# An encoder block on one NeuronCore: the input projection in seven block products, its side work put into 224 slots by hand

## The chip, the core and the metric

The kernel runs on one core of a Trainium2 chip. The metric is the device time of one execution in microseconds; the kernel before took 1524.46 us (median of three runs, 1522.24 to 1525.68). Engines: TensorE (matmul, PE in the profile, its weight loads PEld), VectorE (DVE), ScalarE (ACT), GpSimd (POOL), SyncE (SP, which issues most DMAs). SBUF is the memory that the engines work in, PSUM holds TensorE's sums in banks of 128 x 512 float32, HBM lies outside.

## The reference, cut to what matters

One block over 2048 tokens of width 1024, all in float32:

```
u    = rms_norm(x, norm_in_g)
proj = u @ w_in                                # (2048, 1024) @ (1024, 4096)
pool_x, pool_z, m_x, m_z = split(proj, 4)      # 1024 columns each
y_pool = pool_mixer(pool_x) * silu(pool_z)     # window means 2, 4, 8, 16, then a 256x256 map per group
c = silu(conv5(m_x) + b);  q, k = headwise(c); v = headwise(m_x)
h = mlstm(q, k, v, gates, forward) + mlstm(..., backward)   # 4 heads, 16 chunks of 128 tokens
y_m = (norm(h) * w + skip * c) * silu(m_z)
out = rms_norm(x + concat(y_pool, y_m) @ w_out, norm_out_g)
```

## The kernel before, in words

Each float32 operand of the projection is split into two reduced-precision parts, hi and lo (`split`, line 89: a cast on ScalarE, a subtraction on VectorE, line 94), and each product is three matmuls: hi x hi, hi x lo, lo x hi.

**Projection** (`project`, line 129). The 4096 columns are 32 blocks of 128, the tokens 4 blocks of 512, the inner width 8 pieces of 128. One (column block, token block) is 24 matmuls into one of four PSUM banks (`psp`). The norm isn't multiplied into x: hi and lo of x times the norm's weight are made as the pieces arrive (lines 217, 218), and `rnorm` is multiplied in when a bank is read (lines 204, 408, 543, 550). So the first matmul needs one piece of x, and the norm of a token block (`squares`, `norm`, `spread`, lines 222 to 248) is needed when its first bank is read.

**Stages.** (1) `load_block` and the first two m_x column blocks. (2) The other six, with the mapping of m_x beside them: `conv` (line 311; five taps on VectorE), Silu, `headwise` (keys and values by token, lines 321 to 340; their transposes, line 344), and `fold` (line 162), which multiplies the pooling map into the pool_x weights. (3) Four m_z blocks with the gate rows. (4) Eight pool_x and eight pool_z blocks with the window sums. (5) The last four m_z blocks with the 15 updates of the backward state of head 0 (`next_backward`, line 622; `update`, line 593, which writes two PSUM banks of one buffer and has VectorE read them) and, in the last pair, the loads of the first half of w_out (`load_out`, line 636). (6) `run` (line 959): 64 steps of the memory with the output projection beside them.

**Order.** In stages 1 to 5 a planner orders each engine's instructions by its own estimate of when they can start. In stage 6 TensorE, VectorE, ScalarE and GpSimd keep the order of the program (`manual_schedule`, line 993); DMA queues are planned throughout.

Of the kernel before, what the change touches and what calls it, by code (L numbers as in the profile page):

```python
# [17 lines left out]
P = 128  # L18
# [3 lines left out]
NB = 4  # L22
# [8 lines left out]
ENG = mybir.EngineType  # L31

# [18 lines left out]
def hymba_block(ctx, tc, xT, x, w_in, wpxT, pool_w, bqT, bkT, bvT, bv, w_g, b_g, par, edge, w_out, g_out, out):  # L51
# [16 lines left out]
    g_s = dram.tile([2, P, P], F32, name="g_s")  # L68
    o_s = dram.tile([S, D], F32, name="o_s")
# [13 lines left out]
    dec_bc = cpool.tile([P, P], F32, name="dec_bc")  # L83
    pga = ExitStack()
# [11 lines left out]

    ph1 = ExitStack()
    rp = open_pool(ph1, "rp", side="right")
    wpool = open_pool(ph1, "wpool", bufs=2, side="right")
    psp = open_pool(ph1, "psp", bufs=4, side="right", space=PSUM)  # L100
    rnorm = rp.tile([P, S], F32, name="rnorm")
    uh, ul = {}, {}
    ub = {b: ExitStack() for b in reversed(range(NB))}
    for b, stack in ub.items():
        up = open_pool(stack, f"u{b}", side="right")
        uh[b] = up.tile([P, KT, BT], F32R, name=f"uh{b}")
        ul[b] = up.tile([P, KT, BT], F32R, name=f"ul{b}")

    def fetch_w(src):
        wl = wpool.tile([P, KT, P], F32, name="wl", bufs=1)  # L110
        nc.sync.dma_start(out=wl, in_=src)
        return wl

    def split_w(wl):
        whi = wpool.tile([P, KT, P], F32R, name="whi")
        wlo = wpool.tile([P, KT, P], F32R, name="wlo")
        split(wl, whi, wlo, nc.vector)
        return whi, wlo

    def load_w(src):  # L120
        return split_w(fetch_w(src))
# [7 lines left out]
    def project(w, b, kts=range(KT), ps=None):  # L129
        whi, wlo = w  # L130
        if ps is None:
            ps = psp.tile([P, BT], F32, name="proj")
        for kt in kts:
            for n, (l, r) in enumerate(((whi, uh[b]), (whi, ul[b]), (wlo, uh[b]))):
                pe(nc.tensor.matmul(ps, lhsT=l[:, kt, :], rhs=r[:, kt, :],  # L135
                                    start=(kt == 0 and n == 0), stop=(kt == KT - 1 and n == 2)))
        return ps


    phw = ExitStack()  # L140
    hwp = open_pool(phw, "hwp", bufs=2, side="right")

    def load_headwise(i):
        t = {}
        for name, src in (("k", bkT), ("v", bvT)):
            t[name] = hwp.tile([P, P], F32, name=f"bl{name}")
            nc.sync.dma_start(out=t[name], in_=src[i])

        t["q"] = hwp.tile([P, P + 48], F32, name="blq")
        nc.sync.dma_start(out=t["q"][:, :P], in_=bqT[i])  # L150
        nc.sync.dma_start(out=t["q"][:, P:].rearrange("p (a b) -> p a b", a=3), in_=w_g[i])
        t["vw"] = hwp.tile([P, 16 + P], F32, name="vw")
        nc.sync.dma_start(out=t["vw"][:, 16:], in_=bv[i])
        return t

    pm = ExitStack()
    mxp = open_pool(pm, "mxp", bufs=2)
    psk = open_pool(pm, "psk", bufs=3, space=PSUM)
    psg = open_pool(pm, "psg", space=PSUM)


    def fold(g):
        pwh = fop.tile([P, 2, HD], F32R, name="pwh", bufs=1)
        pwl = fop.tile([P, 2, HD], F32R, name="pwl", bufs=1)
        for ct in range(2):
            pw = fop.tile([P, HD], F32, name="wt", bufs=2)
            nc.sync.dma_start(out=pw, in_=pool_w[g][:, ct, :])
            split(pw, pwh[:, ct, :], pwl[:, ct, :], nc.gpsimd, nc.gpsimd)

        def parts(kt):  # L170
            wt = fop.tile([P, 2, P], F32, name="wt", bufs=2)
            nc.sync.dma_start(out=wt, in_=wpxT[g][:, :, kt * P:(kt + 1) * P])
            wh = fop.tile([P, 2, P], F32R, name="wh")
            wl = fop.tile([P, 2, P], F32R, name="wlf")
            split(wt, wh, wl, nc.gpsimd, nc.gpsimd)
            return wh, wl

        nxt = parts(0)
        yield
        for kt in range(KT):  # L180
            wh, wl = nxt
            ps = psk.tile([P, 2, P], F32, name="hw")
# [4 lines left out]
            st = fop.tile([P, 2, P], F32, name="st", bufs=1)  # L187
            nc.scalar.copy(st, ps)
            nc.scalar.dma_start(out=wp_s[2 * g:2 * g + 2, :, kt, :].rearrange("c p n -> p c n"), in_=st)
            if kt + 1 < KT:  # L190
                nxt = parts(kt + 1)
            yield

    def new_mx(pool):
        mx = pool.tile([P, S + 4], F32, name="mx")
        nc.gpsimd.memset(mx[:, :2], 0.0)
        nc.gpsimd.memset(mx[:, S + 2:], 0.0)
        return mx

    ws, hw, mxs = [], [], []  # L200

    def evac_mx(i, b, ps):
        bt = slice(b * BT, (b + 1) * BT)
        nc.vector.tensor_tensor(mxs[i][:, 2 + b * BT:2 + (b + 1) * BT], ps, rnorm[:, bt], op=ALU.mult)  # L204

    with ExitStack() as pro:
        xq = open_pool(pro, "xq", bufs=2)


        def load_block(b):  # L210
            xts = []
            for kt in range(KT):
                g = par_sb[:, kt, 9:10]
                xt = xq.tile([P, BT], F32, name="xt", bufs=12)
                xts.append(xt)
                nc.sync.dma_start(out=xt, in_=xT[b][:, kt, :])
                nc.scalar.activation(uh[b][:, kt, :], xt, AF.Copy, scale=g)
                nc.vector.scalar_tensor_tensor(ul[b][:, kt, :], in0=xt, scalar=g,  # L218
                                               in1=uh[b][:, kt, :].bitcast(F32), op0=ALU.mult, op1=ALU.subtract)
                yield xts  # L220

        def squares(xts):
            sm = None
            for k in range(KT // 2):
                sq = [xq.tile([P, BT], F32, name="sq", bufs=6) for e in range(2)]
                nc.gpsimd.tensor_tensor(sq[0], xts[2 * k], xts[2 * k], op=ALU.mult)
                nc.scalar.activation(sq[1], xts[2 * k + 1], AF.Square)
                (nc.gpsimd if k < 2 else nc.vector).tensor_tensor(sq[0], sq[0], sq[1], op=ALU.add)
                if sm is not None:
                    nc.vector.tensor_tensor(sq[0], sq[0], sm, op=ALU.add)  # L230
                sm = sq[0]
            return sm

        def norm(b, sm):
            ss = psg.tile([P, 512], F32, name="pg")
            for i in range(4):
                nc.tensor.matmul(ss[:, i:i + 1], lhsT=sm[:, i * P:(i + 1) * P], rhs=ones[:, 0:1], start=True, stop=True)
            rs = mxp.tile([P, 4], F32, name="rs")
            nc.vector.tensor_scalar(rs, ss[:, 0:4], 1.0 / D, EPS, op0=ALU.mult, op1=ALU.add)
            nc.gpsimd.tensor_tensor(rs, rs, mhalf, op=ALU.pow)  # L240
            return rs

        def spread(b, rs):
            rb = psg.tile([P, BT], F32, name="pg")
            for i in range(4):
# [10 lines left out]
        for b in range(NB):  # L256
            load = load_block(b)
            pss = [psp.tile([P, BT], F32, name="proj") for i in range(2)]
            for kt in range(KT):
# [12 lines left out]
                if kt == 3 and late:  # L272
                    late.pop()()
# [775 lines left out]
```

## Time and profile before

| | |
|---|---|
| three runs | 1522.24, 1524.46, 1525.68 us |
| profiled execution | 1520.88 us, its span 1519.2 us |
[...]
| projection (stages 1 to 5) | until 859 us of the span |

The page gives the busy time of each engine and the chain of work that ended last. A matmul's own duration (0.39 us for 512 columns) overlaps the next one's; the distance from start to start is its pitch. A row of the timeline gives start, duration, engine, line, operation, tiles and, in brackets, how long the engine was idle before it and who ended that. "x4" merges four instructions.

### The profile page before, as it was taken

The numbers are of one execution on the slowest core, as the hardware profiler recorded it, in microseconds if no ns is written. First come the engines' busy times: TensorE is split into PE (matmuls) and PEld (weight loads), VectorE is DVE, ScalarE is ACT, GpSimd is POOL, SyncE is SP. The second block draws the span as 40 slices with busy tenths as digits, with TensorE's granted clock in tenths as the row PEclk, the third lists the DMA queues.
The fourth block names the chain that finished last, engine by engine and source line by source line (L and its number), as shares of the span: only waits on it lengthen the run. The fifth ranks groups of instructions, "written<-read, shape, count | busy, mean of one in ns | idle before, by whom it ended". The sixth has DMA issues, their size and how long they took to land.

```text
span 1519.2 us, 21070 instructions
## 1 busy us (share of the span) xinstructions
PE 1493.2 (98%) x7193; PEld 1259.9 (83%) x7193; DVE 845.6 (56%) x1700; ACT 494.6 (33%) x1144; POOL 359.8 (24%) x549
## 2 busy tenths in 40 slices
PE   8899999999999999999999999999999999999998
PEld 6788888878888888888888878888888888888886
DVE  8896355563133333445433377767777777665553
ACT  6344433343110011011112444444344445433331
POOL 5544333310000210222200123233332323121100
PEclk8999999999999999999999999999999999999999
DMA  6268765552201111111053787877777778765442
GB/s 223 66 201 234 211 181 169 167 164 80 77 14 56 56 44 53 56 56 44 26 159 107 225 245 233 234 228 207 224 223 216 222 211 262 200 194 156 139 135 84
DMA packets 251339, 231.11 MB, mean 152 GB/s; under 512 B 18400, under 2 KB 211168, under 8 KB 250208
## 3 DMA queue, kind: packets, MB, share of 16 engines
q1 hardware_dynamic: 236768, 215.08, 47.9%
q10 hardware_dynamic: 14464, 14.68, 3.0%
q8 instruction: 57, 0.93, 0.3%
q14 instruction: 50, 0.41, 0.1%
HBM read 149.81 MB, written 79.89 MB: 151 GB/s over the span
## 4 chain that ended last, share of the span: by engine, by line
PE 91%; DVE 3%; DMA 3%; ACT 1%; POOL 1%; issue 1%; SPq 0%; DVEq 0%; POOLq 0%; ACTq 0%
PE proj L135 42%; PE po L685 23%; PE upd L597 7%; PE num L817 7%; PE hw L336 4%; PE num L812 4%; PE sT L802 2%; PE hw L185 1%; PE py L869 1%; DVE ul L218 1%; PE hw L344 1%; DVE c L316 1%; DMA kk<-kk_s 1%; DMA xt<-in_xT 1%; DMA wost<-in_w_out 1%
## 5 line engine op out<-in xcount | busy, mean ns | idle before, releaser
L135 PE MATMUL proj<-uh,whi 128*128 128x512 f32 x1024 | 407.7, 398 | 3.7 <-DVE mx L204 2.3
L135 PE MATMUL proj<-ul,whi 128*128 128x512 f32 x1024 | 402.3, 393 | 2.1 <-DVE ul L218 2.1
L135 PE MATMUL proj<-uh,wlo 128*128 128x512 f32 x1024 | 402.5, 393 | 0.0
L135 PEld LDWEIGHTS proj<-uh,whi 128*128 128x128 f32 x1024 | 194.4, 190 | 43.1 <-DVE mx L204 2.4
L135 PEld LDWEIGHTS proj<-ul,whi 128*128 128x128 f32 x1024 | 194.1, 190 | 41.8 <-DVE ul L218 2.4
L135 PEld LDWEIGHTS proj<-uh,wlo 128*128 128x128 f32 x1024 | 193.9, 189 | 41.2
L685 PE MATMUL po<-woh,yh 128*128 128x512 f32 x512 | 217.6, 425 | 0.0
L685 PE MATMUL po<-woh,yl 128*128 128x512 f32 x512 | 201.5, 394 | 0.0
L685 PE MATMUL po<-wol,yh 128*128 128x512 f32 x512 | 201.3, 393 | 0.0
L597 PE MATMUL upd<-v,kw 128*128 128x258 f32 x480 | 124.2, 381 | 3.1 <-ACT hh L833 1.9
L791 POOL TENSOR_TENSOR cw<-cT,gw 128x512 f32<-128x512 f32 (+1 forms) x64 | 79.0, 1234 | 168.5 <-issue 77.9
L685 PEld LDWEIGHTS po<-woh,yl 128*128 128x128 f32 x512 | 96.2, 188 | 22.1
L685 PEld LDWEIGHTS po<-wol,yh 128*128 128x128 f32 x512 | 96.6, 189 | 19.2
L685 PEld LDWEIGHTS po<-woh,yh 128*128 128x128 f32 x512 | 96.4, 188 | 19.1
L91 ACT CAST whi<-wl 128x1024 fp32r<-128x1024 f32 x31 | 32.6, 1052 | 229.0 <-PE proj L135 225.9
L316 DVE SCALAR_TENSOR_TENSOR c<-mx,par_sb,c 128x512 f32<-128x512 f32 x128 | 103.6, 827 | 3.0
L597 PEld LDWEIGHTS upd<-v,kw 128*128 128x128 f32 x480 | 87.3, 190 | 14.9 <-ACT hh L833 2.0
L543 DVE TENSOR_TENSOR ux<-proj,rnorm 128x512 f32<-128x512 f32 x32 | 22.1, 692 | 124.7 <-PE proj L135 124.7
L784 POOL TENSOR_SCALAR_AFFINE_SELECT gw<-gw 128x128 f32<-128x128 f32 x128 | 43.8, 365 | 172.6 <-DMA gw<-g_s 170.5
L875 ACT ACTIVATE yt<-cT,par_sb 128x128 f32<-128x128 f32 x128 | 44.5, 394 | 108.8 <-DMA ym_s<-yt 108.7
L851 POOL TENSOR_TENSOR rstd<-rstd,mhalf 128x1 f32<-128x1 f32 x64 | 35.1, 549 | 174.5 <-DVE rstd L849 99.8
L833 ACT ACTIVATE hh<-num,rn 128x256 f32<-128x256 f32 x64 | 30.1, 471 | 141.9 <-DVE rn L829 133.8
(194 smaller groups left out, 2184.5 us busy)
## 6 DMA issues: line engine op xcount, KB each, us to landing
gw<-g_s SPq DMA_DIRECT2D x128, 128.0 KB, 4.8
v<-v_s SPq DMA_DIRECT2D x124, 129.0 KB, 4.5
kk<-kk_s SPq DMA_DIRECT2D x124, 128.0 KB, 4.0
wl<-in_w_in SPq DMA_DIRECT2D x23, 512.0 KB, 3.8
xt<-in_xT SPq DMA_DIRECT2D x32, 256.0 KB, 4.8
cT_s<-c SPq DMA_DIRECT2D x32, 256.0 KB, 3.7
kk_s<-tokst SPq DMA_DIRECT2D x32, 256.0 KB, 2.5
kkT_s<-kkTb SPq DMA_DIRECT2D x32, 256.0 KB, 4.1
```

What stands on the lines that cost most here:

```text
L91: nc.scalar.copy(hi, src)
L135: pe(nc.tensor.matmul(ps, lhsT=l[:, kt, :], rhs=r[:, kt, :], start=(kt == 0 and n == 0), stop=(kt == KT - 1 and n == 2)))
L316: nc.vector.scalar_tensor_tensor(c, in0=mx[:, b * BT + t:(b + 1) * BT + t], scalar=par_sb[:, i, t:t + 1], in1=c, op0=ALU.mult, op1=ALU.add)
L336: nc.tensor.matmul(ps[:, e, :], lhsT=src[:, o:o + P], rhs=rhs, start=True, stop=True)
L597: pe(nc.tensor.matmul(ps[:, m, :E], lhsT=t["kw"][:, ms], rhs=t["v"], start=True, stop=True))
L685: pe(nc.tensor.matmul(ps, lhsT=l[:, kt, :], rhs=r, start=(kt == 0 and e == 0), stop=(kt == 7 and e == 2)))
L784: nc.gpsimd.affine_select(out=a["gw"][:, 0, d, :], in_=a["gw"][:, 0, d, :], compare_op=ALU.is_ge, fill=BIG, base=0, pattern=[[pat, P]], ch ...
L791: eng.tensor_tensor(a["cw"][:, ds], a["cT"][:, None].broadcast_to([P, nd, 2, P]), a["gw"][:, 1, ds, None, :].broadcast_to([P, nd, 2, P]), ...
L812: pe(nc.tensor.matmul(num[:, d, :E], lhsT=a["dd"][:, d, :], rhs=a["kv"]["v"], start=True, stop=d not in a["dirs"]))
L817: pe(nc.tensor.matmul(num[:, d, :E], lhsT=a["cw"][:, d, m, :], rhs=state[:, m, :], start=False, stop=(m == 1)))
L851: nc.gpsimd.tensor_tensor(a["rstd"][:, 0:1], a["rstd"][:, 0:1], mhalf[:, :1], op=ALU.pow)
L875: nc.scalar.activation(a["yt"][:, m, :], a["cT"][:, m, :], AF.Copy, scale=par_sb[:, i, 8:9])
```

## The change

The tokens become two halves of two blocks of 512, the inner width two halves of 512, and two column blocks are taken together: a 2x2x2 of blocks. Such a unit needs eight block products; seven products of sums and differences (P1 to P7) give the same four result blocks. There are 16 units (`plan`: four m_x pairs, one m_z pair, eight pool pairs (x and z of one block), three m_z pairs) in each of two halves of the tokens: 2 x 16 x 7 = 224 slots of one product (12 matmuls) each. P1, P6, P7 and P4 add up in one bank, P5 and P3 in another, P2 stands alone; banks are read in the slot after their product, three of them copied (`snap`) to be added elsewhere.

The combinations of x (seven operands of 512 x 512, hi and lo) stay in SBUF for a half: 14 tiles. So that they can be formed, the norm is now multiplied into x first (`scale_x`). The combinations of weights are made for every unit in both halves, sums on GpSimd, hi on ScalarE, lo on VectorE. All other work is attached to slots (`at_slot`): "top", "pre", "mid" (between the second and third quarter of the product) and "end". Four engines keep this order throughout. Convolution and pooling run in halves with a halo kept over (`mt_s`, `uxt`, `szt`); the second half maps its tokens in chunks of 384. The maps `mv` go to HBM and come back in the second half. `fold` splits with ScalarE and GpSimd where it used GpSimd alone, and `ob` has four buffers where it had two.

```diff
+    PRODUCTS = ("P1", "P5", "P6", "P2", "P7", "P3", "P4")
+    def load_raw(u):
...
+            raw[u, e] = ap.tile([P, KT, P], F32, name=f"w{e}")
+            nc.sync.dma_start(out=raw[u, e], in_=t)
+    def sum_a(u, k):
...
+        nc.gpsimd.tensor_tensor(sums[k], x, y, op=op_)
+    def prepare_a(u, k):
...
+        split(v[k] if k in v else sums[k], hi, lo, nc.vector)
+    def product(k, put, middle):
...
+        bank = "x" if k == "P2" else "z" if k in ("P5", "P3") else "y"
...
+        for q in range(4):
+            if q == 2:
+                middle()
+            for n, (l, r) in enumerate(((ah, bh), (ah, bl), (al, bh))):
+                pe(nc.tensor.matmul(ps, lhsT=l[:, q, :], rhs=r[:, q, :], ...
+        if k in ("P1", "P5", "P6"):
+            pending.append(lambda: snap(k, ps))
+        elif k == "P4":
+            pending.append(lambda: put(1, 0, ps, None))
+        else:
+            e, t, other = {"P2": (0, 0, "P1"), "P7": (1, 1, "P5"), "P3": (0, 1, "P6")}[k]
+            pending.append(lambda: put(e, t, ps, snaps[other]))
+    def squares(t, kt):
+        sq = ob.tile([P, BT], F32, name="op")
+        nc.scalar.activation(sq, xs[t, kt], AF.Square)
...
+            nc.vector.tensor_tensor(rn[t], rn[t], sq, op=ALU.add)
+    def scale_x(t, kt):
+        nc.vector.scalar_tensor_tensor(xs[t, kt], in0=xs[t, kt], scalar=par_sb[:, kt, 9:10], in1=rn[t], ...
+    def prepare_b(k):
...
+        for q in range(4):
+            x11, x12, x21, x22 = xs[0, q], xs[1, q], xs[0, 4 + q], xs[1, 4 + q]
+            v = {"P1": x11, "P5": x11, "P6": x11, "P2": x21, "P7": x12, "P3": x22, "P4": x21}[k]
+            if k in ("P5", "P6", "P7", "P4"):
+                x, y = {"P5": (x12, x11), "P6": (x22, x11), "P7": (x22, x12), "P4": (x21, x11)}[k]
+                (nc.vector if k in ("P5", "P6") else nc.gpsimd).tensor_tensor(v, x, y, op=ALU.subtract)
+            split(v, hi[:, q], lo[:, q], nc.vector)
+    SUMS = {3: "P5", 4: "P6", 5: "P7", 6: "P3"}
+    NEXT = {3: ("P1",), 4: ("P5",), 5: ("P6", "P2"), 6: ("P7",)}
+    OWN = {0: "P3", 1: "P4"}
+    def slot(g):
...
+        run_events(g, "top")
...
+        read_banks()
+        if k in OWN:
+            prepare_a(u, OWN[k])
+        if nxt and k == 1:
+            load_raw(nxt)
+        if nxt and k in SUMS:
+            sum_a(nxt, SUMS[k])
+            for x in NEXT[k]:
+                prepare_a(nxt, x)
+        run_events(g, "pre")
+        product(PRODUCTS[k], puts[U], lambda: run_events(g, "mid"))
+        run_events(g, "end")
...
+            for s, c in zip(range(6) if p else (0, 1, 3, 5), chunks):
+                at_slot(g + s, "pre", conv, p, *c)
+                at_slot(g + s + 1, "pre", conv_silu, p, *c)
+                at_slot(g + s + 2, "mid", headwise, p, *c, 0)
+                at_slot(g + s + 2, "end", headwise, p, *c, 1)
+                at_slot(g + s + 3, "mid", keys_across, p, *c)
...
+    E0 = UNITS * SLOTS
+        at_slot(E0 - 12 + kt // 2, "pre", squares, 1, kt)
+        at_slot(E0 - 7 + kt // 4, "pre", scale_x, 1, kt)
...
+    for k, s in zip(PRODUCTS, (1, 3, 4, 5, 7, 9, 10)):
+        at_slot(E0 - 7 + s, "pre", prepare_b, k)
+    for s in range(6):
+        at_slot(s, "end", fold_steps, 2)
...
+    schedule = tc.manual_schedule(engines={ENG.PE, ENG.DVE, ENG.Activation, ENG.Pool})
+    with schedule:
+        fold_steps(1)
...
+        load_x(xq[0], 0, 0)
+        load_raw(plan[0])
+        load_x(xq[1], 0, 1)
+        for kt in range(KT):
+            squares(0, kt)
+            fold_steps(1)
+        norm_sums(xq[0], 0)
+        norm_spread(0)
+        prepare_a(plan[0], "P1")
+        for k in ("P5", "P6", "P7"):
+            sum_a(plan[0], k)
+        for kt in range(4):
+            scale_x(0, kt)
+        prepare_b("P1")
+        for kt in range(KT):
+            squares(1, kt)
+        norm_sums(xq[1], 1)
+        norm_spread(1)
+        fold_steps(2)
+        for kt in range(4):
+            scale_x(1, kt)
+        for k in ("P5", "P6", "P2", "P7"):
+            prepare_a(plan[0], k)
...
+        for g in range(2 * E0 - 15):
+            slot(g)
...
+        for g in range(2 * E0 - 15, 2 * E0):
+            k = g - (2 * E0 - SLOTS)
+            if k < 0:
+                slot(g)
                 next_backward()
+                next_backward()
+                continue
...
+            slot(g)
+            bstack[PRODUCTS[k]].close()
+            room(k)
```

In the first slots `prepare_b` of P5, P6, P2 with P7, and P3 with P4 stand in slots 0, 1, 2 and 3; the other eight `scale_x` stand behind P5's in slot 0. `room` opens the SBUF that the closed operands leave, and loads and splits the first quarter of w_out and the first y there.

## Rows read from the trace of the kernel before

**Rows 1.** The page: busy time by engine, then the last chain by engine.
```profile
PE 1493.2 (98%) x7193; PEld 1259.9 (83%) x7193; DVE 845.6 (56%) x1700; ACT 494.6 (33%) x1144; POOL 359.8 (24%) x549
...
PE 91%; DVE 3%; DMA 3%; ACT 1%; POOL 1%; issue 1%; SPq 0%; DVEq 0%; POOLq 0%; ACTq 0%
```

**Rows 2.** Windows: length, PE, PEld, DVE, ACT, POOL busy, clock, DMA share, GB/s.
```profile
400.00:500.00 100.00, 100.00 (x443) 82.81 (x442) 32.89 (x30) 11.97 (x16) 7.61 (x8) 1.00 0.12 40
```

**Rows 3.** Timeline of projection alone: start, duration, engine, line, operation.
```profile
500.13 0.39 PE L135 MATMUL proj<-ul,whi 128*128 128x512 f32 x1
...
505.57 0.39 PE L135 MATMUL proj<-ul,whi 128*128 128x512 f32 x1
```

**Rows 4.** Timeline of TensorE: 12 fold products; 8 values, 4 transposes, projection again.
```profile
200.69 0.28 PE L185 MATMUL hw<-pwh,wh 128*128 128x256 f32 x1
...
202.12 0.39 PE L135 MATMUL proj<-uh,whi 128*128 128x512 f32 x1
...
205.86 1.14 PE L336 MATMUL hw<-vw,mx 128*128 128x144 f32 x8
206.84 0.60 PE L344 MATMUL hw<-ident,tokst 128*128 128x128 f32 x4
207.20 0.48 PE L135 MATMUL proj<-uh,whi 128*128 128x512 f32 x1
207.52 0.39 PE L135 MATMUL proj<-ul,whi 128*128 128x512 f32 x1
```

**Rows 5.** Windows of line 135 alone, then line 336 alone: the first 100 us.
```profile
0.00:100.00 100.00, 71.28 (x264) 53.95 (x264) 0.91 0.49 153
...
0.00:100.00 100.00, 4.11 (x30) 3.89 (x31) 0.91 0.49 153
```

**Rows 6.** Start: timeline of TensorE, then a window (PE busy, clock, DMA, GB/s).
```profile
10.50 0.63 PE L135 MATMUL proj<-uh,whi 128*128 128x512 f32 x1
10.93 0.63 PE L135 MATMUL proj<-ul,whi 128*128 128x512 f32 x1
...
10.00:15.00 5.00, 5.00 (x13) 0.51 1.05 396
```

**Rows 7.** Timeline of the first norm: power, spread.
```profile
27.12 1.46 POOL L240 TENSOR_TENSOR rs<-rs,mhalf 128x4 f32<-128x4 f32 x1 [1.36 <-DVE rs L239]
...
32.41 1.05 PE L246 MATMUL pg<-ident,rs 128*128 128x128 f32 x8
```

**Rows 8.** Groups by form: busy, mean ns of one, idle before: two lo parts.
```profile
L94 POOL TENSOR_TENSOR wlf<-wt,wh 128x256 fp32r<-128x256 f32 x32 | 30.6, 955 | 2.6
...
L94 DVE TENSOR_TENSOR wol<-wost,woh 128x512 fp32r<-128x512 f32 x32 | 23.0, 721 | 17.0 <-ACT woh L91 14.7 <-DMA sz_s<-op 2.2
```

**Rows 9.** Timeline: VectorE alone, and beside a GpSimd operation; three scalings alone.
```profile
19.42 0.68 DVE L230 TENSOR_TENSOR sq<-sq 128x512 f32<-128x512 f32 x1
19.57 1.42 POOL L226 TENSOR_TENSOR sq<-xt 128x512 f32<-128x512 f32 x1 [1.89 <-DVE sq L228]
20.02 1.52 DVE L228 TENSOR_TENSOR sq<-sq 128x512 f32<-128x512 f32 x1
...
59.60 2.06 DVE L218 SCALAR_TENSOR_TENSOR ul<-xt,par_sb,uh 128x512 fp32r<-128x512 f32 x3
```

**Rows 10.** Convolution: line 316 (ns min/median/max), and the group of its first step.
```profile
L316 DVE SCALAR_TENSOR_TENSOR c<-mx,par_sb,c x128: 733/753/1226, 75.7 to 314.5; 128x512 f32<-128x512 f32 x128
...
L314 DVE TENSOR_SCALAR c<-mx,par_sb 128x512 f32<-128x512 f32 x32 | 18.2, 573 | 9.9 <-PE hw L336 5.2 <-DMA wt<-in_wpxT 3.5 <-ACT c L318 0.8
```

**Rows 11.** Timeline: an update that waited for the one before; line 603's reading.
```profile
881.14 1.14 PE L597 MATMUL upd<-v,kw 128*128 128x258 f32 x4 [1.20 <-DVE cb L600]
...
L603 DVE SCALAR_TENSOR_TENSOR cb<-cb,dec_bc,upd x56: 741/752/753, 771.2 to 1247.0; 128x516 f32<-128x516 f32 x56
```

**Rows 12.** Timeline of ScalarE: a cast that waited for its load.
```profile
872.96 0.62 ACT L91 CAST woh<-wost 128x512 fp32r<-128x512 f32 x1 [3.80 <-DMA wost<-in_w_out]
```

**Rows 13.** Waits of TensorE: total us, times, longest.
```profile
PE hw L336 <- ACT tokst L337: 3.6, 3, 2.1
```

More of the change, by code (lines that the diff above doesn't have):

```diff
@@ L94, in split @@
         lo_eng.tensor_tensor(lo, src, hi.bitcast(F32), op=ALU.subtract)
-    ph1 = ExitStack()
[L98 to L121, printed above, removed]
+    PRODUCTS = ("P1", "P5", "P6", "P2", "P7", "P3", "P4")
+    keep = ExitStack()
+    kp = open_pool(keep, "kp")
+    uxt = kp.tile([P, 8, 16], F32, name="uxt")
+    szt = kp.tile([P, 8, 8], F32, name="szt")
+    ed = kp.tile([P, len(EDGE)], F32, name="ed")
+    nc.sync.dma_start(out=ed, in_=edge.partition_broadcast(P))
+    ph1 = ExitStack()
+    ap = open_pool(ph1, "ap", side="right")
+    psp = open_pool(ph1, "psp", side="right", space=PSUM)
+    bstack = {k: ExitStack() for k in reversed(PRODUCTS)}
+    bpool = {k: open_pool(stack, f"b{k}", side="right") for k, stack in bstack.items()}
+    B, A, raw, sums = {}, {}, {}, {}
     ordered = []
@@ L127, in pe @@
         return tc.keep_in_program_order(ins) if ordered else ins
[L129 to L137, printed above, removed]
@@ L140, in hymba_block @@
[L140 to L154, printed above, removed]
@@ L181, in fold @@
             wh, wl = nxt
+            if kt + 2 < KT:
+                load(kt + 2)
+            if kt + 1 < KT:
+                nxt = parts(kt + 1)
             ps = psk.tile([P, 2, P], F32, name="hw")
@@ new lines, in put_mx, with put @@
+    def put_mx(p, u):
+        def put(e, t, ps, other):
+            i = 2 * u[1] + e
+            if i not in made:
+                new_mx(p, i)
+                made.add(i)
+            a = at(p, p * S // 2 + t * BT)
+            dst = mxs[i][:, a:a + BT]
+            if other is None:
+                nc.scalar.copy(dst, ps)
+            else:
+                nc.vector.tensor_tensor(dst, ps, other, op=ALU.add)
+            if p == 0 and t == 1:
+                nc.sync.dma_start(out=mt_s[i], in_=mxs[i][:, FIRST:])
+        made = set()
+        return put
@@ new lines, in hymba_block, with open_m, open_z, open_x @@
+    left = {}
+    def open_m(p):
+        nonlocal mxp, sp, hwp
+        pm = left["m"] = ExitStack()
+        hwp = open_pool(pm, "hwp", bufs=2, side="right")
+        mxp = open_pool(pm, "mxp")
+        sp = open_pool(pm, "sp")
+    def open_z():
+        nonlocal zp
+        left["z"] = ExitStack()
+        zp = open_pool(left["z"], "pp", bufs=2)
+    def open_x(t):
+        left["x", t] = ExitStack()
+        xq[t] = open_pool(left["x", t], f"xq{t}")
+    def fold_steps(n):
+        for _ in range(n):
+            next(folds, None)
```

630 lines of the change are left out of this document (351 added, 279 removed).

## The prediction

> **What bounds the kernel now.** Read the page first: busy time, then the chain that ended last. TensorE is busy 98% of the span and the chain runs on it for 91%, on VectorE for 3% [rows 1]. Busy time overstates a pipelined engine, so look next at a stretch with projection alone: 100 us hold 443 products of 512 columns at clock 1.00 [rows 2], and the timeline there has 24 from one start to the next like it in 5.44 us, 0.2267 us each [rows 3]. VectorE, ScalarE and GpSimd have 33, 12 and 8 us of work in those 100 us [rows 2]. So before 860 us the time is the number of products times their pitch, plus what TensorE does between them, plus its waits. Most of the waits are at the front: in the first 100 us it issues 264 projection products (59.8 us) and 30 for keys and values (3.7 at 0.98/8) [rows 4, 5], and by their pitches 12 folds (1.4) [rows 4] and 64 norm products (8.4 at 1.05/8) [rows 7]; 73 of 100 us, so 27 are lost, partly to waits and partly to the half clock after them (pitch 0.43, granted clock 0.51) [rows 6].
>
> **The change, part by part.** Times are against the profiled execution, 1520.9 us (span 1519.2), which lies 3.6 below the median of the three runs, 1524.5; at the end I add 3.6.
>
> *Products.* Before: 32 column blocks x 4 token blocks x 8 x 3 = 3072. After: 16 pairs x 2 halves x 7 products x 12 = 2688. 384 x 0.2267 = **-87.1 us** [rows 3]. TensorE does everything else as often as before. Their pitch stays: same operands, banks of the same size, weight loads still under them.
>
> *The front.* Before, the first product needs one raw piece of x, and the norm is multiplied in on the way out. After, it needs the whole norm of 512 tokens, and the second product that of 1024. Step by step. (a) x, two weights and the first fold pieces are some 5.3 MB; at 396 GB/s [rows 6] and a start at 2.5 us they land by about 16 to 18 us, and fold pieces queued behind them are waited for by ScalarE, whose order is now written out, so about two of the eight squares are done by 18 us. (b) Each further square stands in line with a fold step: a split lo on GpSimd (0.96) [rows 8], six products (0.72 at full clock [rows 4], 1.3 at half), copies: some 1.9 us each, six of them: 29 us. (c) The norm is serial: add, sums (8 products, taken as long as the spread), power 1.46, spread 1.05 [rows 7], copy, handovers: 6 us, to 35. (d) VectorE then has 4 scalings at 0.66 [rows 9], 5 lo parts and 8 adds at 0.61 to 0.72 [rows 8], 11 us to 46; the second norm to 52; folds that now stand ahead of the first product in TensorE's order to 56; product 1 at half clock, 12 x 0.43, to 61. (e) P5 and P6 need per quarter a subtraction on VectorE, a cast on ScalarE (0.62) [rows 12] and the lo part on VectorE, in this order with nothing between: 0.68 + 0.62 + 0.68, 2.0 us, where 12 products of a whole slot take 2.7. Two operands are 16 us, eight scalings between them 5, lo parts of the pair's own weights 3, the other four operands 10: the last is ready at about 94, and unit 0 ends at about 100 us. By then TensorE has done 84 products (19 us), 23 fold steps (16.4) and some 5 of norms and maps: 40, so 60 lost against 27: **+33 us**. Below: without the cast waits (-6), with every transfer in time (-8), +18. Above: the folds at the ends of the first slots also wait behind those casts, +45.
>
> *The second half's operands.* They are made between slots 105 and 115 (E0 = 112), beside products. VectorE from slot 105 on: 3.4, 6.4, 0, 8.6 (P5), 9.3 (P6) us for slots of 2.72. P7's bank is read behind all of this, at about 27.7 after the start of slot 105, and P4, which adds to that bank, would have started at 16.3: 11.4 late, and a restart below full clock (12 x 0.2 = 2.4): **+13**. Low end 5 (no cast waits), high 20 (GpSimd sums between).
>
> *Backward updates.* Fifteen ran with 12 products between; now two stand behind each of 8 slots, on one PSUM buffer, so the second waits until VectorE has read the first. The nearest row is an update that waited 1.20 for that [rows 11], and the reading alone is 0.75. 7 pairs x 1.2 = **+8.5**; 3 if other tails cover it, 10 at most.
>
> *Keys and values.* 40 chunks in place of 32 blocks, each entered from two places of a slot. A return to 512 columns costs 0.32 in place of 0.227 [rows 4]: 80 - 32 returns x 0.1 = **+5** (2 to 8).
>
> *The last unit.* Loading w_out and the first y moves between products whose banks ScalarE also reads. ScalarE waited 3.80 for one such load [rows 12]; here it blocks the copies of P6 and the reading of P7. One such wait less the slot of slack, twice: **+5** (0 to 12).
>
> *Convolution, gates.* VectorE has work for 25 us in a convolving unit of the second half (below) and TensorE 31, so I charge only spikes: **+4** (0 to 25, the rival). The three waits for ScalarE in the old mapping stage, 3.6 [rows 13], go: **-4**.
>
> SP: weights are fetched twice, 32 MB for 16, and each slot-1 load waits for P4's weights; there are two slots until they are wanted, and DMA is at 0.12 in that stage [rows 2]. Nothing.
>
> Sum: -87.1 + 33 + 13 + 8.5 + 5 + 5 + 4 - 4 = **-22.6**: 1498.3 in the profile's frame, **1502** by the median.
>
> **VectorE against GpSimd.** Two VectorE additions of one shape took 0.68 and 1.52 us; the second began while a 1.42 us GpSimd operation ran [rows 9]. [...] The sum holds without this; it speaks for the second rival.
>
> **Rivals.**
> 1. *The fills are hidden.* If the front costs +18, the second fill +5 and the rest its low ends (3 + 2 + 0 + 0 - 4), the gain is 63: 1461. For it: VectorE's bare work at the front is near 46 us. Against it: two serial norms of 6 us, and an order that puts folds ahead of the first product.
> 2. *VectorE becomes the bound of the eight convolving units: slower.* A 512-token convolution is a first step of 0.57 and four steps of pitch p [rows 10]. Second half, per unit: 6 chunks of 384 tokens, 2.6 + 18p; 7 lo parts with their cast, 9.1; 3 readings, 2.1: 13.8 + 18p, against TensorE's 7 x 2.72 + 18 blocks x 0.58 + 1.2 = 30.7. First half: 13.2 + 14p against 27.9. At p = 0.66 VectorE fits. Over the eight units the excess is 128p - 126; from p = 1.19 on it eats the gain and 3 us more, and at 1.44 (1.52 less overlap) it is +58: 1556. For it: contended steps reach 1.226. Against it: their median is 0.753 with GpSimd in play [rows 10].
> 3. *Each of the 224 slots costs something at its start.* A bank handed over and a new operand could cost 0.1 us, as a return does [rows 4]: 22 us, and no change: 1524. Against it: a change of bank and weights every 24 products costs nothing in 443 products [rows 2]. This is also the way in which seven products would not be cheaper than eight.
> 4. *Front, second fill and last unit all at their upper ends*, +31 on the sum: 1533.
>
> **Chances.** Forecast 0.45 (its own range 1484 to 1520); rival 1, 0.28; rival 2, 0.14; rival 3, 0.07; rival 4, 0.06. About 0.2%, 3 us, is what a measurement here tells from no change. Faster 0.73, within it 0.07, slower 0.20. The range 1466 to 1532 leaves out part of rival 1's best end and most of rival 2.
>
> **What would show it.** The products of 512 columns in front of the output stage count 2688 at 0.227. The first starts after 50 us, and unit 0 ends near 100. TensorE waits some 10 us for VectorE about slot 111, and 1.2 us seven times in front of an update. A first product before 40 us, or no wait at slot 111, makes the forecast wrong towards rival 1; a mean convolution step above 1.2 us, or TensorE waiting in every slot, towards rivals 2 and 3.

## The result, and the profile after

The changed kernel is slower: 1639.59 us (median, 1635.4 to 1642.36) against 1523.35 in runs beside it, ratio 1.0761 [1.0731, 1.0791], 116 us. The forecast was 1502. The profiled execution has a span of 1637.6 us, 118.4 above that of the kernel before.

The page of the changed kernel: span, busy time by engine, TensorE's busy share and granted clock in 40 slices of 41 us, the last chain by engine.

```profile
span 1637.6 us, 21563 instructions
...
PE 1466.2 (90%) x6809; PEld 1218.6 (74%) x6809; DVE 1037.0 (63%) x2006; ACT 672.6 (41%) x1566; POOL 534.0 (33%) x699
...
PE   5359899999876699888998879999999999999998
...
PEclk6578999999897899988999999999999999999999
...
PE 48%; DVE 4%; DMA 2%; ACT 1%; issue 1%; SPq 0%; ACTq 0%; POOL 0%; DVEq 0%; POOLq 0%
```

TensorE has 384 instructions fewer than in [rows 1], yet its busy share fell from 98 to 90%. The slices under 90% say where: 1 to 3 and 5 (to 205 us), 11 to 14 (409 to 573), 17 to 19 (655 to 778), 22 to 24 (860 to 983). Windows of the same kernel (columns as in [rows 2]):

```profile
290.00:390.00 100.00, 100.00 (x443) 82.81 (x442) 56.91 (x65) 34.22 (x62) 53.16 (x47) 1.00 0.28 97
0.00:67.00 67.00, 29.48 (x106) 23.76 (x107) 21.19 (x33) 22.57 (x46) 17.99 (x24) 0.57 0.39 124
520.00:540.00 20.00, 2.20 (x5) 1.81 (x6) 12.61 (x15) 6.66 (x12) 8.27 (x5) 0.54 0.07 26
```

With nothing in its way the projection runs at the pitch of before: 443 products in 100 us, as in [rows 2]. In the first 67 us no engine is half busy: none of them is full, they wait for each other. TensorE's waits in 0 to 150, 390 to 580 and 890 to 1000 us (total us, times, longest; `hw` is the bank of a fold or a mapping, `pg` that of the norm sums, `psx`, `psy` and `psz` those of the products):

```profile
PE hw L274 <- ACT wh L97: 41.7, 11, 8.5
PE pg L205 <- DVE rn L200: 14.0, 2, 13.2
...
PE psy L171 <- DVE op L394: 21.2, 2, 19.6
PE pg L205 <- DVE rn L200: 13.1, 2, 9.2
PE psy L171 <- DVE mx L383: 5.6, 1, 5.6
...
PE upd L797 <- ACT kw L791: 10.5, 8, 2.8
PE po L884 <- ACT yh L97: 8.2, 1, 8.2
```

All losses together: for each TensorE instruction the time to the next start, less the pitch that its shape has when TensorE runs freely (0.227 us for 512 columns, 0.119 for 256, 0.122 for 144 and so on). Waits and a low clock (0.57 and 0.54 in the windows above) are both in it. A "unit" is 1/32 of the projection's products; at "the turn" the operands of the second half of the tokens are made. "Planned" is a run told of below (x8).

```
us lost on TensorE        before   after   planned
unit 0                      11.6    93.3     54.5
units 1 to 7                18.5    25.6     16.9
units 8 to 16 (the turn)     3.8    57.7     28.1
units 17 to 20               0.0     9.4      5.0
units 21 to 24 (gates)       0.0    19.7     14.0
units 25 to 29               0.3     7.7      9.1
units 30, 31                 0.0    14.5     14.2
output stage                11.6    23.4     25.0
sum                         45.8   251.3    166.8
```

The sums differ by 205.5 us; less the 87.1 of the 384 products that is 118.4, the difference of the two spans. That they agree is arithmetic, since the free pitches of the two kernels differ by the 384 products alone. That the saving came in full is shown by the pitch in 290 to 390 us; waits and the low clock took more than twice as much.

Two places show how. First slot 0 (start, duration, engine, line, operation, wait), where the operand of P5 is made:

```profile
73.56 0.68 DVE L230 TENSOR_TENSOR x<-x,x 128x512 f32<-128x512 f32 x1
74.27 0.62 ACT L97 CAST bhP<-x 128x512 fp32r<-128x512 f32 x1 [1.93 <-DVE x L230]
74.92 0.69 DVE L100 TENSOR_TENSOR blP<-x,bhP 128x512 fp32r<-128x512 f32 x1 [0.68 <-ACT bhP L97]
...
80.20 0.62 ACT L97 CAST bhP<-x 128x512 fp32r<-128x512 f32 x1 [1.36 <-DVE x L230]
80.72 0.40 ACT L97 CAST wh<-wt 128x256 fp32r<-128x256 f32 x1
81.17 0.58 PE L274 MATMUL hw<-pwh,wh 128*128 128x256 f32 x1 [8.43 <-ACT wh L97]
...
95.93 0.58 PE L274 MATMUL hw<-pwh,wh 128*128 128x256 f32 x1 [8.46 <-ACT wh L97]
```

A fold's cast of 0.40 us stands in ScalarE's order behind four operand casts, each of which waits for VectorE; the fold's product stands in TensorE's order ahead of the next slot. The same a slot later. (These two waits are the longest of the first slots, but x1 and x2 show below that they are not what the folds cost.) Second the turn:

```profile
526.13 0.68 DVE L230 TENSOR_TENSOR x<-x,x 128x512 f32<-128x512 f32 x1
...
527.90 6.72 POOL L230 TENSOR_TENSOR x<-x,x 128x512 f32<-128x512 f32 x4
528.41 1.75 DVE L230 TENSOR_TENSOR x<-x,x 128x512 f32<-128x512 f32 x1
...
535.10 0.68 DVE L230 TENSOR_TENSOR x<-x,x 128x512 f32<-128x512 f32 x1
...
537.07 0.68 DVE L394 TENSOR_TENSOR op<-psy,P 128x512 f32<-128x512 f32 x1
537.80 0.80 PE L171 MATMUL psy<-bhP,ahP 128*128 128x512 f32 x1 [19.64 <-DVE op L394]
```

P4 waits 19.64 us until VectorE has read P7's bank, a reading of 0.68 that stands behind two whole operands. In both fences work that was ready stood behind work that was not: the last product into P7's bank started at 515.05 us and the bank was read at 537.07; the load for the fold's cast was issued before 68.5 us (2.6 us to landing at most), and the cast started at 80.72.

### The profile page after: what moved, and what is told of

It is laid out like the page before. It is cut to its first block, busy times and chain, and to the rows that moved or that the text cites. A ratio compares the mean times of both kernels' runs of the same rounds, so it can differ in the third digit from the quotient of the medians.

```text
span 1637.6 us, 21563 instructions
## 1 busy us (share of the span) xinstructions
PE 1466.2 (90%) x6809; PEld 1218.6 (74%) x6809; DVE 1037.0 (63%) x2006; ACT 672.6 (41%) x1566; POOL 534.0 (33%) x699
## 4 chain that ended last, share of the span: by engine, by line
PE 48%; DVE 4%; DMA 2%; ACT 1%; issue 1%; SPq 0%; ACTq 0%; POOL 0%; DVEq 0%; POOLq 0%
PE po L884 21%; PE num L1016 6%; PE upd L797 6%; PE psy L171 5%; PE num L1011 3%; PE psz L171 3%; PE sT L1001 2%; PE py L1068 1%; PE psx L171 1%; DMA kk<-kk_s 1%; DMA y<-yp_s 1%; DVE alP L100 1%; DMA sz_s<-op 0%; ACT ahP L97 0%; DMA ym_s<-yt 0%
## 5 line engine op out<-in xcount | busy, mean ns | idle before, releaser
L171 PE MATMUL psy<-bhP,ahP 128*128 128x512 f32 x512 | 216.6, 423 | 43.4 <-DVE op L394 24.5
L100 DVE TENSOR_TENSOR alP<-sum,ahP 128x512 fp32r<-128x512 f32 x128 | 119.6, 936 | 140.0 <-ACT ahP L97 140.0
L171 PE MATMUL psy<-blP,ahP 128*128 128x512 f32 x512 | 207.5, 405 | 0.0
L171 PE MATMUL psy<-bhP,alP 128*128 128x512 f32 x512 | 207.3, 405 | 0.0
L171 PEld LDWEIGHTS psy<-bhP,ahP 128*128 128x128 f32 x512 | 101.5, 198 | 68.3 <-DVE op L394 26.2
L797 PE MATMUL upd<-v,kw 128*128 128x258 f32 x480 | 125.7, 385 | 11.3 <-ACT kw L791 10.5
L171 PEld LDWEIGHTS psy<-bhP,alP 128*128 128x128 f32 x512 | 100.8, 197 | 22.8
L171 PEld LDWEIGHTS psy<-blP,ahP 128*128 128x128 f32 x512 | 101.4, 198 | 19.0
L330 DVE SCALAR_TENSOR_TENSOR c<-mx,par_sb,c 128x384 f32<-128x384 f32 (+1 forms) x160 | 110.5, 690 | 5.6
L171 PE MATMUL psz<-bhP,ahP 128*128 128x512 f32 x256 | 106.7, 417 | 0.0
L171 PE MATMUL psz<-blP,ahP 128*128 128x512 f32 x256 | 102.8, 402 | 0.0
L171 PE MATMUL psz<-bhP,alP 128*128 128x512 f32 x256 | 102.6, 401 | 0.0
```

What stands on the lines that cost most here:

```text
L100: lo_eng.tensor_tensor(lo, src, hi.bitcast(F32), op=ALU.subtract)
L171: pe(nc.tensor.matmul(ps, lhsT=l[:, q, :], rhs=r[:, q, :], start=(first and q == 0 and n == 0), stop=(q == 3 and n == 2), skip_group_check ...
L330: nc.vector.scalar_tensor_tensor(c[:, :m], in0=mx[:, o + t:o + t + m], scalar=par_sb[:, i, t:t + 1], in1=c[:, :m], op0=ALU.mult, op1=ALU.add)
L797: pe(nc.tensor.matmul(ps[:, m, :E], lhsT=t["kw"][:, ms], rhs=t["v"], start=True, stop=True))
```

## The experiments

The first theory: too much work stands between the norm and the operands, and the folds' casts behind it. Its rivals are in the expectations. "Changed" is the changed kernel, 1.0761; every ratio is to the kernel before.

**Folds, second half's operands, operand chain (x1 to x4).**

```
x1   squares(0, kt)                       # fold_steps taken out of the front
     for s in range(5, 26): at_slot(s, "mid", fold_steps, 1); if s > 6: at_slot(s, "end", fold_steps, 1)
x2   no fold_steps;  (wp_s[i], w_in[8 + i]) -> (w_in[i], w_in[8 + i])
x3   - load_x, squares, norm_sums, norm_spread, scale_x, prepare_b at E0 - 42 ... E0 + 3
x4   prepare_b:  for q: subtract, cast, low  ->  for q: subtract; for q: cast; for q: low
```

> The 36 fold steps leave the front and the first five slots; they go one to the middle and one to the end of slots 5 to 25. Theory (folds stand ahead of products in the written order, and each waits for a ScalarE cast that is queued behind the casts of the operands): of the 82 us that TensorE lost in the first 118 us about 40 go, and of the 23 us lost in the folds of 118 to 200 us some 15 go; the 16 us of fold products done in the front are paid later. Sum -40, 1600 us, ratio to the kernel before about 1.05. Rival (the front is the serial chain norm, scaling, operands; the folds only fill its gaps): the chain keeps its length, and the folds' 16 us move from an idle stretch to a busy one: 1655 us, ratio 1.086.

1629.58 us, 1.0700 [1.0680, 1.0719]: neither. The first product starts at 36.8 us for 67.5 and the 84th at 94.9 for 133.2, so the folds did hold the front by 38 us. Of these, 30.7 lie ahead of the first product: ScalarE's copy of the first norm comes at 18.6 us, in the changed kernel at 43.66. From the first product to the 84th it took 58.2 us for 65.8, with 6 fold products between them for 66; less 0.119 for each that is 57.5 and 57.9 (and 57.5 in x2, with none). So the two waits of 8.4 us were no price: without the folds TensorE waits in the same two slots for the operands of P6 and P5 themselves (first two lines, 0 to 95 us). By product 336 only 14.7 of the 38 us is left. The folds' 23 us of products are now beside projection products, and they wait there too (third line, ScalarE's waits, 95 to 215 us):

```profile
PE psy L171 <- ACT bhP L97: 10.0, 1, 10.0
PE psz L171 <- ACT bhP L97: 5.9, 1, 5.9
...
ACT st L277 <- DMA wp_s<-st: 26.9, 16, 4.9
```

> Leaves out the folding of the pool weights into the projection altogether, so the eight pooled column blocks use unfolded weights. It prices everything that hangs on the folds. Theory of the folds: as the run with the folds moved, and 192 fold products of 0.119 us (23 us) less, about 1575 us, ratio 1.034. Rival of the serial chain: only the 7 us of fold products that stood after 118 us and their 23 us of waits there go, the front stays: 1615 us, ratio 1.06.

1577.53, 1.0360 [1.0342, 1.0379]: the theory's number. The folds cost 62 us in the written order, 23 of products and 39 of waits.

> Leaves out the second half's x loads, squares, norms, scalings and operands: the second half uses the operands of the first half. It prices the second fill. Theory (VectorE's written order at the turn of the halves is the wait): the 54 us that TensorE lost between 390 and 580 us go, but for some 4: 1590 us, ratio 1.043. Rival (VectorE is slowed by GpSimd's sums and pooling at this place anyway, or the bank reads are late without the fill): at most half of it goes, 1612 us or more, ratio 1.06.

1580.37, 1.0379 [1.0362, 1.0397]: the theory; 59 us hang on the second half's operands, with their norms and scalings, 46 more than the forecast had.

> Each operand is made by kind: its four subtractions first, then four casts, then four low parts, in place of subtraction, cast, low part for each quarter in turn. Theory (the chain VectorE, ScalarE, VectorE per quarter is serial): P5 and P6 take 5.4 to 6.1 us in place of 7.9, twice per half, so about 4 us at the front and 4 to 5 at the turn: 1631 us, ratio 1.070. Rival (their time is set by contention with GpSimd and by ScalarE's queue, not by the chain): no change, 1639 us, ratio 1.076.

1625.95, 1.0684 [1.0668, 1.0700]: 13.6 us, somewhat more than expected. An operand now takes 4.9 us of VectorE without a gap:

```profile
72.87 2.48 DVE L232 TENSOR_TENSOR x<-x,x 128x512 f32<-128x512 f32 x4
75.28 2.48 DVE L236 TENSOR_TENSOR blP<-x,bhP 128x512 fp32r<-128x512 f32 x4
```

**Repairs inside the written order, and the order itself (x5 to x8).**

```
x5   st = fop.tile(..., name="st")  ->  st = ob.tile([P, BT], F32, name="op")[:, :2 * P]
x6   x1 + x4 + x5;  slot(g); next_backward(); next_backward()
       ->  at_slot(g, "mid", next_backward); slot(g); next_backward()
x7   x4;  P5, P6 at the turn in two pieces: quarters 0, 1 at "end" of a slot, 2, 3 at "mid" of the next
x8   with schedule:  ->  with ExitStack():       # slots 0 to 208: the planner orders
```

> The fold's result is copied into the four buffers of the op pool in place of the single buffer st, so ScalarE's copy no longer waits until the store before it has landed. In the changed kernel ScalarE stood 14 times for 24.3 us in all on that wait in the first 205 us, 18 of them behind the 118th. Theory (the folds that come after the front are late because ScalarE stands in front of that store, with the casts of the next fold and the copies of the banks behind it): 15 to 18 us less, 1623 us, ratio 1.066. Rival (the folds wait for the load of their weights and for the casts, and the store only fills that time): 1637 us, ratio 1.075.

1631.94, 1.0708 [1.0687, 1.0728]: 8 us, between the two. The wait for the store went; the fold products still waited 39.9 us for their casts in the first 205 us.

> Four edits at once: the folds in slots 5 to 25, their results in four buffers, each operand made by kind, and the second of each pair of backward updates moved into the middle of its slot. If they add: -10 (folds moved), -14 (by kind), -15 (store) and -8 (updates, from eight waits of 1.2 us) make 1592 us, ratio 1.045. If they share one idle stretch (the fold edits are two ways to the same waits): 1605 us, ratio 1.054.

1597.53, 1.0489 [1.0470, 1.0509]: between the two, nearer to adding: 42 us. Still 75 above the kernel before.

> By kind, and at the turn of the halves the operands P5 and P6 are made in two pieces each, at the end of one slot and in the middle of the next, so that VectorE reads a bank between the pieces. Theory (P4 waits because P7's bank is read behind two whole operands in VectorE's order): the wait of 15.3 us in front of P4 in the by-kind run falls to about 6, and the time from 1626 to 1617 us, ratio 1.062. Rival (VectorE has more work in these twelve slots than they last, so what is taken away at P4 returns as a wait for an operand or for another bank): 1626 us, ratio 1.068.

1626.55, 1.0688 [1.0668, 1.0708], as with x4 alone: the rival. P4's wait fell from 15.1 to 12.6 and the time did not. VectorE's pieces follow each other without a gap, and the bank is read behind the low parts of the last piece:

```profile
516.08 2.36 DVE L232 TENSOR_TENSOR x<-x,x 128x512 f32<-128x512 f32 x2
518.37 3.42 DVE L236 TENSOR_TENSOR blP<-x,bhP 128x512 fp32r<-128x512 f32 x2
521.71 0.68 DVE L398 TENSOR_TENSOR op<-psy,P 128x512 f32<-128x512 f32 x1
```

> The same program for the projection, with its order on TensorE, VectorE, ScalarE and GpSimd left to the planner in place of the order written out, up to slot 208. Theory (too much work of VectorE and ScalarE stands between the norm and the operands, and the number of buffers sets the rest): the time changes by less than 15 us, 1625 to 1655 us, ratio 1.067 to 1.086. Rival (the written order as such puts waiting work ahead of work that is ready): the planner takes back 40 us or more, 1600 us or less, ratio under 1.05.

1555.97, 1.0222 [1.0206, 1.0239]: 84 us, and my theory falls. The same instructions on the same buffers, in an order by planned start times, take back most of the loss. Waits of TensorE in this run, 0 to 150 us, then 390 to 580 us:

```profile
PE hw L274 <- ACT wh L97: 6.1, 2, 4.7
...
PE psy L171 <- DVE op L394: 7.8, 1, 7.8
```

Against the fence of the changed kernel: 41.7 us for fold casts became 6.1, the norm's 14.0 and 13.1 are gone, P4's wait is 7.8. The first product starts at 24.3 us for 67.5, the 84th at 92.7 for 133.2: what the planner gains by then it gains ahead of the first product. VectorE's order at the turn now has bank readings (line 394) among the operand's pieces:

```profile
456.32 1.76 DVE L230 TENSOR_TENSOR x<-x,x 128x512 f32<-128x512 f32 x1
458.01 0.68 DVE L394 TENSOR_TENSOR op<-psx,P 128x512 f32<-128x512 f32 x1
458.61 1.38 DVE L100 TENSOR_TENSOR alP<-sum,ahP 128x512 fp32r<-128x512 f32 x1
```

**Which part of the order (x9, x10), and what it leaves (x11, x12).**

```
x9   planned: front and slots 0 to 27      written: slots 28 to 208
x10  written: front and slots 0 to 27      planned: slots 28 to 208
x11  x8 + x4 + x5 + the updates of x6
x12  x11 + folds as in x1
```

> The planner orders the front and slots 0 to 27, the written order holds from slot 28 on. In the run with all of it planned, product 336 of 2688 started 44 us earlier than in the changed kernel, and 34 of the rest came between products 1176 and 1428, at the turn of the halves. If the front's gain is the order of the front alone: 1639 - 44 = 1595 us, ratio 1.047. Rival (what the front gains is given back where the written order takes over, since its work waits there): above 1615 us, ratio 1.061.

1595.74, 1.0485 [1.0457, 1.0513]: -44, as expected.

> The written order holds for the front and slots 0 to 27, the planner orders slots 28 to 208. If the gains of the two parts add: 84 - 44 = 40 us, nearly all at the turn of the halves: 1599 us, ratio 1.050. Rival (the turn gains only what a kernel that is early already leaves): under 20 us, 1620 us or more, ratio 1.064.

1603.47, 1.0539 [1.0523, 1.0555]: -36, as expected. The two parts add to 80 of the 84. Each run keeps the waits of its written part, the first line x9 from 390 to 580 us, the second x10 from 0 to 150:

```profile
PE psy L171 <- DVE op L394: 21.3, 2, 19.7
```

```profile
PE hw L274 <- ACT wh L97: 40.0, 11, 8.5
```

> All of slots 0 to 208 planned, and three edits: operands by kind, fold results in four buffers, second backward update in the middle of its slot. TensorE's waits in the planned run give the prices: updates 9.6 us, fold stores 5.7, operands for products P1, P5, P2 (casts and low parts) about 16. If by kind and the store matter as little as the planner lets them: 1556 - 8 = 1548 us, ratio 1.017. If they add as in the written order (-14, -8, -8): 1526 us, ratio 1.002.

1560.86, 1.0252 [1.0237, 1.0267]: a miss by both; 5 us slower than x8. The planner now puts the first product at 47.3 us for 24.3.

> As the run before, and the fold steps written into slots 5 to 25 in place of the front, so that the planner has products first in the program and folds as what can fill. If the folds at the front cost even the planner (TensorE waited 18 us for fold casts, low parts and copies there): 10 us less than the run with three, about 1538 us, ratio 1.010. Rival (the planner uses the folds to fill waits at the front that are there anyway, and they then take time among products): 10 us more than the run with three, 1558 us, ratio 1.023.

1562.85, 1.0269 [1.0252, 1.0286]: nearer to the rival; the intervals of the two runs overlap, so where the folds are written makes no difference to the planner that these runs can tell. The four repairs that gave the written order 42 us give the planned one nothing.

**What still holds the planned version (x13 to x18).**

```
x13  x8 + x3        x14  x8, and the last 15 slots planned too
x15  planned: slots 0 to 27, 98 to 125, 148 to 173; written: the rest
x16  x8 without squares, norm_sums, norm_spread, scale_x of the first half
x17  x8 + x2        x18  x14 + updates of x6 + snap("P6") by nc.vector.tensor_copy
```

> Slots 0 to 208 planned, and the second half uses the first half's operands (its x, norms, scalings and operands are left out). In the written order this took away 59 us. If the planner already hides what can be hidden, what is left between products 1176 and 1428 (76.6 us for 57.2 us of products) goes: 19 us, 1537 us, ratio 1.010. Rival (the whole second fill still costs as in the written order, spread thin): 1556 - 59 = 1497 us, ratio 0.984.

1531.42, 1.0059 [1.0044, 1.0074]: near the theory. The second half's operands cost 25 us planned, 59 written. VectorE has that work in either order, so 34 of the 59 are put down to the order.

> The planner orders the last 15 slots of the projection too, so nothing ahead of the output stage has a written order. TensorE waited there in the planned run 9.6 us for updates, 4.6 for banks and 7.9 for the first y. If these are the written order again: about 12 us of the 22 go, 1544 us, ratio 1.015. Rival (they are loads of keys, of w_out and of y that arrive late, and one bank for two updates): 1554 us or more, ratio 1.021.

1553.28, 1.0206 [1.0184, 1.0229]: the rival. The order of the last slots is worth 3 us at most.

> The planner orders slots 0 to 27, 98 to 125 and 148 to 173 (front, turn, gates), the written order holds in 28 to 97, 126 to 147 and 174 to 208. In the wholly planned run P7 waited 15 times for ScalarE's copy of P6's bank, 19.9 us in all, nine of them in stretches that are written here, where the changed kernel had next to none. If those go and the rest stays: 1556 - 13 = 1543 us, ratio 1.014. Rival (the waits in front of convolution and norm sums of the written order come back): 1565 us, ratio 1.028.

1574.52, 1.0342 [1.0324, 1.0359]: the rival, and worse than it. The waits for the copies fell from 19.9 us to 7.4 (first line, after 200 us), but the norm sums' and others came back:

```profile
PE psy L171 <- ACT P L154: 7.4, 3, 3.3
PE psy L171 <- DVE sz L427: 5.7, 5, 2.1
PE pg L205 <- DVE rn L200: 5.1, 2, 3.9
```

> Slots 0 to 208 planned; the first half leaves out squares, norm sums, spread and the scaling of x, so its operands come from x as loaded. It prices the norm at the front. If the front is the serial chain of two norms and scalings: the 84th product, at 92.7 us in the planned run, comes 20 us earlier, 1536 us, ratio 1.009. Rival (the front is ScalarE's and VectorE's casts and low parts of operands and folds, at half clock): under 8 us, 1548 us or more, ratio 1.018.

1552.26, 1.0195 [1.0180, 1.0210]: the 84th product comes 25 us earlier, even more than the theory had, and the end only 4, as its rival had it. Unit 0 lost 17 us less (37.7 for 54.5), units 2 and 3 16 more (22.8 for 6.5). In x8, 102 fold products stood in front of the 84th projection product, here 60; the folds that had filled the norm's waits now stand among projection products and wait there (67 to 200 us):

```profile
PE hw L274 <- ACT st L277: 10.0, 8, 2.6
```

> Slots 0 to 208 planned, the folding of the pool weights left out (the pooled column blocks use unfolded weights). The folds are 192 products of 0.119 us, 23 us. With TensorE's waits for fold casts, low parts and copies in the planned run (6.1, 6.1 and 5.7 us) and the half clock behind them: 1556 - 23 - 18 = 1515 us, ratio 0.995; without the norm nothing was gained because the folds stood there, so then they are the front's bound. Rival (the planner hides all but their products): 1533 us, ratio 1.007.

1527.39, 1.0040 [1.0024, 1.0056]: 29 us for the folds, 23 of products and 6 of waits: nearer to the rival. They aren't the front's bound by themselves. Unit 0, which here ends at 81 us, still loses 54.0 us. VectorE is busy 44.8 of the 50 us before 75:

```profile
25.00:50.00 25.00, 14.93 (x47) 11.31 (x47) 21.17 (x31) 10.13 (x21) 8.70 (x4) 0.60 0.20 66
50.00:75.00 25.00, 15.14 (x45) 9.89 (x46) 23.67 (x26) 14.70 (x31) 14.03 (x9) 0.73 0.14 39
```

> All of the projection planned, the second backward update in the middle of its slot, and the copy of P6's bank made by VectorE in place of ScalarE. In the wholly planned run P7 waited 13 times, 16.6 us, for that copy, which stood on ScalarE behind a cast that waited for GpSimd's sum of the next pair's weights. If VectorE is free to copy: -16, and -5 from the updates, 1532 us, ratio 1.006. Rival (VectorE's order has a low part of the same sum ahead of the copy, and waits for the same cast): 1548 us, ratio 1.017.

1550.87, 1.0193 [1.0178, 1.0208]: the rival. The wait changed its engine and grew, from 16.6 us for ScalarE's copy to 25.7 for VectorE's:

```profile
PE psy L171 <- DVE P L154: 25.7, 15, 4.8
```

In x14 the copy stood here on ScalarE, behind a cast that waited for GpSimd's sum, which waited for its weights:

```profile
721.67 1.29 POOL L140 TENSOR_TENSOR sum<-w 128x512 f32<-128x512 f32 x1 [1.96 <-DMA w<-in_w_in]
...
724.36 0.62 ACT L97 CAST ahP<-sum 128x512 fp32r<-128x512 f32 x1 [0.75 <-POOL sum L140]
724.88 0.58 ACT L154 COPY P<-psy 128x512 f32<-128x512 f32 x1
...
725.51 0.50 PE L171 MATMUL psy<-bhP,ahP 128*128 128x512 f32 x1 [1.30 <-ACT P L154]
```

No version beats the kernel before, not even those that leave work out. Where the 116 us went: 84 are the written order. The other 33 (1556 against 1523) are 121 us more lost on TensorE than before, less the 87 saved: 43 in unit 0, 24 at the turn, 42 in units 17 to 31, 13 in the output stage. Shown for these: the turn is the second half's operands (x13), and the order of the last slots isn't their cause (x14). The rest is open. In unit 0, leaving out the norm or the folds gives back 4 and 6 us beyond the folds' products. VectorE is nearly full there in x17, which speaks for its low parts and scalings as the bound, or for GpSimd's work beside them (at the turn of the changed kernel a subtraction took 1.75 us beside GpSimd's and 0.68 else); no run took either away. In units 17 to 31 the longest waits of the planned run are those for ScalarE's copies, which x15 and x18 moved but did not remove. In the output stage it is the 7.7 us for the cast of the first y; no run loaded it earlier.

## Why the prediction was wrong, step by step

- **Products**, -87.1: right, by the count and the pitch. Rival 3 (a price per slot) is out: no loss in 290 to 390 us, 37 slots.
- **The front**, +33: the step that failed most. Unit 0 lost 93.3 us where 60 were forecast, and the 27 set against them are the losses of the first 100 us of the kernel before, whose unit 0 lost 11.6: +82 in place of +33. Two stretches were sized too short (lines below).
  - Steps (a) to (c), up to the first norm: it was there at 44.2 us for 35. In ScalarE's order the squares stand behind fold casts, and three of these waited 1.5, 4.8 and 8.6 us for their loads; without the folds x1 has the norm at 19.2. From there the second norm's sums stand ahead of P1 in TensorE's order and held it 13.2 us, though P1's operand was whole at 50.9; the first product came at 67.5 for 56. The forecast took this order as given; the planner does not keep it and starts at 24.3.
  - Step (e): from the first product to the 84th it took 66 us for 44. P5 and P6 were sized rightly (8.0 us each, 8 expected), but the low parts of the other four operands took 18.5 us of VectorE where 10 were forecast: six of the sixteen took 1.75 or more, beside GpSimd's work, where one takes 0.68. The last was ready at 120.3 for 94.
  - "Above: the folds at the ends of the first slots also wait behind those casts, +45": they did, 8.43 and 8.46 us, but by x1 and x2 this cost no more than the folds' own products. The folds' price lay ahead of the first product (30.7 us) and behind the 84th. x9 prices the order of this whole part at 44 us, x2 the folds in all at 62.

```profile
23.22 0.40 ACT L97 CAST wh<-wt 128x256 fp32r<-128x256 f32 x1 [8.55 <-DMA wt<-in_wpxT]
...
43.66 0.59 ACT L215 COPY rn<-pg 128x512 f32<-128x512 f32 x1 [4.90 <-PE pg L213]
...
48.41 2.48 DVE L100 TENSOR_TENSOR blP<-x,bhP 128x512 fp32r<-128x512 f32 x4
...
56.85 1.86 PE L205 MATMUL pg<-ones,rn 128*128 128x1 f32 x8 [13.23 <-DVE rn L200]
...
67.48 0.63 PE L171 MATMUL psy<-bhP,ahP 128*128 128x512 f32 x1
...
100.14 9.31 DVE L100 TENSOR_TENSOR blP<-x,bhP 128x512 fp32r<-128x512 f32 x8 [3.85 <-ACT bhP L97]
```

- **The second half's operands**, +13: right mechanism, wrong size: 54 by the table, 59 by x3. P4's wait was 19.6, forecast 11.4: VectorE's scalings began 3.0 us into slot 105, behind the second norm, and two subtractions took 1.75 us beside GpSimd in place of 0.68. The bigger miss is what the sum didn't have: TensorE's norm sums, eight tiny products, stand in order ahead of others and held them 13.1 us; other bank readings took another 8.
- **Backward updates**, +8.5: right. Of the 10.5 us in eight waits above, 2.8 come behind the last product and 1.2 at the first update; the rest, with 0.8 that the profile lists apart, are 7.3 us in front of the second update of seven pairs. The profile names ScalarE's keys there, but each of the seven started 0.10 us after VectorE's reading of the bank had ended, as forecast.
- **Keys and values**, +5 and -4: the first about right: 91 returns to 512 columns cost 9.6 us more than their pitch, for 22 and 2.0 before. The second came the other way: TensorE waited 10.0 us for the mapping's ScalarE operations, for 3.6 before.
- **Convolution, gates**, +4 (0 to 25): units 17 to 24 lost 29. VectorE is not the bound of the convolving units: a step of 384 columns took 619 ns in the median, and the 1.19 us for 512 columns, from which rival 2 decides, are 0.89 for 384. Units 21 to 24 lost 20 of the 29; the gate chain stands there ahead of two products (2.5 and 3.1 us) and of a bank reading (4.6).
- **Last unit**, +5 (0 to 12): units 30 and 31 lost 14.5, some 8 of it at the updates; the output stage 11.8 more than before, 8.2 of it one wait for the cast of the first y.
- **Rival 4** named the right places and was priced at +31 on the sum (its three places alone add to 26: 12, 7 and 7). The truth was +137, because each term was sized as one wait and not with the queue behind it.

VectorE beside GpSimd was slow at the turn too, as in [rows 9]: the subtraction took 1.75 us beside GpSimd's 6.72 and 0.68 both before and after it, the low part 0.99 for 0.69. Two subtractions and three low parts took some 3 us more there; the low parts at the front, 18.5 us for 10, are the larger case.

What none of the steps and rivals had is a rival for the written order as such: I sized each chain as if all other work could go on beside it, which holds only for an order that is free. x8, with the same instructions and buffers in a planned order, prices that at 84 us.

## What to carry to other kernels

In a written order price work by what stands behind it on every engine that it stops: fold casts ahead of the squares, and folds and a second norm ahead of the first product, moved that product from 24 to 67 us. A long wait is not yet a price: the two of 8.4 us for a fold's cast gave nothing back when the folds were gone, since TensorE then waited for the next operand. Before repairing such an order piece by piece, let the planner order the same program once: here four repairs gave 42 us and that one line 84. A saving on the bound engine (87 us) is only there if each fill (front, turn, gates) fits beside the shorter stretch that is left, so add up the fills first.

## Not expected of the hardware

- TensorE's granted clock was low in the two windows in which it was kept waiting: 0.57 over the first 67 us, with TensorE busy 29.48 of them, and 0.54 in 520 to 540 us, busy 2.20 of 20; it was 1.00 in 290 to 390, busy throughout. The wait of 19.6 us cost more than itself: the product behind it took 0.80 us for 0.39, and the next nine started 0.43 us apart in place of 0.227.
- One buffer for a fold's result kept ScalarE 26.9 us in 16 waits for its own stores, up to 4.9 us each (x1), with every cast and bank copy behind them.
